# A streaming log-sum-exp: fifteen loads for seventeen, a larger first load, and late row sums on VectorE

## The chip, the core and the metric

The kernel runs on one core of a Trainium2 chip. The metric is device time in microseconds (us) of one execution: the median of the kernel before is 162.71 us over 3 runs (162.2 to 162.76).

A core has engines that run their own instruction lists side by side and meet at semaphores: TensorE (PE), VectorE (DVE), ScalarE (ACT), GpSimd (POOL) and SyncE (SP). Here SP issues every DMA, ScalarE computes exponentials and logarithms, VectorE sums, and TensorE does two tiny matmuls at the end. Sixteen DMA engines move the data between HBM and the on-chip memory SBUF; PSUM is a second, smaller on-chip memory.

## The reference

```python
def setup_inputs():
    batch, seq, dim = 32, 512, 1024
    return {"x": np.random.randn(batch, seq, dim).astype(np.float32), "axis": -1}

def reference(x, axis):
    x_max = np.max(x, axis=axis, keepdims=True)
    return (x_max.squeeze(axis) + np.log(np.sum(np.exp(x - x_max), axis=axis))).astype(np.float32)
```

There are 16,384 rows of 1024 float32 values, 67.1 MB, and one number comes out of each row.

## The kernel before

Each of the 128 partitions holds 128 consecutive rows of the input. "A row" below means one row in every partition: 128 x 1024 values, 0.52 MB. The kernel streams the 128 rows through a ring of 51 rows in SBUF (`ring`, `RING_ROWS`).

It takes a short cut: it computes log(sum(exp(x))) without subtracting the maximum, and then checks that every sum lay between `LOW` and `HIGH`. If one did not, a second pass (lines 320 to 343) does the work again with the maximum subtracted. With this input the second pass does not run; each engine only tests a verdict and branches to the end.

The list `CHUNKS` (lines 10 to 15) sets the order of the work. Each entry is one load: its rows, how many of them VectorE sums, into how many pieces ScalarE's exp of these rows is cut, and whether VectorE sums by halves. The loop of line 213 goes through the list:

- SP issues the load into the next free rows of the ring (`load`, line 135). Before it does, it waits until the engines that last used those rows are done. A load that does not fit before the end of the ring starts at row 0.
- ScalarE waits until the load has landed and computes exp in place (line 235), for all rows of a piece in one instruction.
- VectorE waits for this exp and sums: with one reduction for the piece (line 255), or, by halves, with one instruction per row that adds the second half of the row to the first and accumulates the sum (line 242, followed by a short read of the accumulator).
- Rows beyond the count for VectorE are summed by ScalarE while it computes exp, row by row (line 262), each followed by an accumulator read.

The loads are of 4, 15, 16, 16, 16, 14, 13, 9, 7, 5, 4, 3, 2, 1, 1, 1 and 1 rows. The last four are "late" rows (`LATE`): ScalarE sums all four, and the sums go to `late` in PSUM; all others go to `sums` in SBUF.

Logarithms are taken in three instructions (`take_logs`, line 157): of 81 columns ahead of the exp of the 9-row load (`LN_AT`, `LN_LAG`), of 43 columns ahead of the last exp (line 221), and of the four late columns at the very end (line 272). SP then stores the first 124 columns (line 276) and the four late ones (line 278). All loads and stores go through one DMA queue, q1. The first load is issued ahead of the barrier with which the program begins (lines 354 to 360).

The check on the sums is VectorE's: the largest and smallest of `sums` (lines 293 and 294), a compare of these with the bounds, a compare of the late columns (line 283, after the last Ln), two matmuls that count the good ones over all partitions (lines 304 and 307), and a reduction to one number (line 312), which SP, ScalarE and VectorE load to decide their branch. At the end SP waits for the stores.

Of the kernel before, what the change touches and what calls it, by code (L numbers as in the profile page):

```python
# [9 lines left out]
CHUNKS = [  # L10
    (4, 4, 1, False), (15, 15, 1, False), (16, 16, 2, False), (16, 16, 2, False),
    (16, 15, 2, False), (14, 14, 2, False), (13, 12, 2, False), (9, 8, 1, False),
    (7, 7, 1, True), (5, 4, 1, True), (4, 3, 1, True), (3, 3, 1, False), (2, 2, 1, True),
    (1, 0, 1, False), (1, 0, 1, False), (1, 0, 1, False), (1, 0, 1, False),
]

CUTS = ()
RING_ROWS = 51


UNEVEN = ()
PARTS = ((0, 128, 2), (1, 128, 4), (3, 128, 8), (7, 64, 8), (71, 128, 8))


LN_AT = 7
LN_LAG = 1


LATE = 4

# [8 lines left out]
def kernel(  # L39
# [6 lines left out]
    nc = tc.nc  # L46
    P = nc.NUM_PARTITIONS
# [4 lines left out]
    N, D = x_flat.shape  # L52
    assert N % P == 0
    NB = N // P
    assert sum(r for r, *_ in CHUNKS) == NB
    assert sum(STEPS) == NB
# [4 lines left out]
    Alu = mybir.AluOpType  # L61
# [4 lines left out]


    assert CHUNKS[-1][0] == 1
    spans = list(zip((0, *CUTS), (*CUTS, D)))
    assert 1 <= len(spans) <= 2  # L70
    n_late = LATE - 1 + len(spans)

# [11 lines left out]
    votes = nc.alloc_psum_tensor("votes", [P, 512], fp32).ap()  # L84
    late = nc.alloc_psum_tensor("late", [P, 512], fp32).ap()

    ALL_GOOD = P * K
    TOO_MANY = 2048.0
    assert TOO_MANY > ALL_GOOD

    landed = [nc.alloc_semaphore(f"landed{i}") for i in range(len(CHUNKS) + len(spans) - 1)]
    act_done = nc.alloc_semaphore("act_done")
# [26 lines left out]
    row = slot = 0  # L119
    for r, *_ in CHUNKS:  # L120
        if slot + r > RING_ROWS:
            slot = 0
        place.append((slot, row))
        slot += r
        row += r
# [8 lines left out]

    def load(i):
        (s, row), r = place[i], CHUNKS[i][0]
        act_wait = max(a for a, _ in busy[s : s + r])
        dve_wait = max(d for _, d in busy[s : s + r])
        if dve_wait:
            nc.sync.wait_ge(dve_done, dve_wait)  # L140
        if act_wait:
            nc.sync.wait_ge(act_done, act_wait)
        dst, src = ring[:, s : s + r], x_v[:, row : row + r]
        if i == len(CHUNKS) - 1:
            for k, (lo, hi) in enumerate(spans):
                nc.sync.dma_start(out=dst[:, :, lo:hi], in_=src[:, :, lo:hi]).then_inc(
                    landed[i + k], 16
                )
        elif i in UNEVEN:
            for first, last, step in PARTS:  # L150
                nc.sync.dma_start(
                    out=dst[first:last:step], in_=src[first:last:step]
                ).then_inc(landed[i], 16)
        else:
            nc.sync.dma_start(out=dst, in_=src).then_inc(landed[i], 16)

# [9 lines left out]

    late_row = place[-LATE][1]
    assert not any(n_dve for _, n_dve, _, _ in CHUNKS[-LATE:])

    def total(t):  # L170
# [3 lines left out]
    n_barrier = len(body.instructions)  # L174
    load(0)
    n_early = len(body.instructions)

# [31 lines left out]
    nc.gpsimd.memset(weights[:, 1:], -TOO_MANY).then_inc(pool_done, 1)  # L209

    logged = 0
    done_before = [(0, 0)]
    for i, (r, n_dve, parts, by_halves) in enumerate(CHUNKS):
        if i:
            load(i)
        s, row = place[i]
        if i == LN_AT:
            logged = place[i - LN_LAG][1]
            take_logs(0, logged, sums[:, :logged], *done_before[i - LN_LAG])
        if i == len(CHUNKS) - 1:  # L220
            take_logs(logged, late_row, sums[:, logged:late_row], *done_before[-LATE])
            early_logs = acts
            for k, (lo, hi) in enumerate(spans):
                nc.scalar.wait_ge(landed[i + k], 16)
                nc.scalar.activation(  # L225
                    out=ring[:, s, lo:hi],
                    in_=ring[:, s, lo:hi],
                    func=Exp,
                    accum_out=late[:, LATE - 1 + k : LATE + k],
                ).then_inc(act_done, 1)  # L230
                acts += 1
            continue
        nc.scalar.wait_ge(landed[i], 16 * (len(PARTS) if i in UNEVEN else 1))
        for lo, hi in cuts(n_dve, parts):
# [5 lines left out]
            if by_halves:  # L240
                for j in range(lo, hi):
                    nc.vector.tensor_tensor_reduce(  # L242
                        out=ring[:, s + j, : D // 2],
                        in0=ring[:, s + j, : D // 2],
                        in1=ring[:, s + j, D // 2 :],
                        scale=1.0,
                        scalar=0.0,
                        op0=Alu.add,
                        op1=Alu.add,
                        accum_out=sums[:, row + j : row + j + 1],  # L250
                    ).then_inc(dve_done, 1)
                    dves += 1
                    busy[s + j] = (0, dves)
            else:
                nc.vector.reduce_sum(  # L255
                    out=sums[:, row + lo : row + hi], in_=ring[:, s + lo : s + hi], axis=AX
                ).then_inc(dve_done, 1)
                dves += 1
                for j in range(lo, hi):
                    busy[s + j] = (0, dves)  # L260
        for j in range(n_dve, r):
# [7 lines left out]
            busy[s + j] = (acts, 0)  # L269
        done_before.append((dves, acts))  # L270

    take_logs(late_row, NB, late[:, : NB - late_row], dves, acts)


    nc.sync.wait_ge(act_done, early_logs)
    nc.sync.dma_start(out=out_v[:, :late_row], in_=res[:, :late_row]).then_inc(stored, 16)
    nc.sync.wait_ge(act_done, acts)
    nc.sync.dma_start(out=out_v[:, late_row:], in_=res[:, late_row:]).then_inc(stored, 16)


    def compare(lo, hi, values):
        nonlocal dves
        nc.vector.tensor_tensor(  # L283
            out=above[:, :, lo:hi],
            in0=values.unsqueeze(1).to_broadcast([P, 2, hi - lo]),
            in1=bounds[:, :, lo:hi],
            op=Alu.is_gt,
        ).then_inc(dve_done, 1)
        dves += 1

    nc.vector.wait_ge(act_done, done_before[-LATE][1])
    nc.vector.wait_ge(dve_done, dves)
    nc.vector.reduce_max(out=ends[:, :1], in_=sums[:, :late_row], axis=AX).then_inc(dve_done, 1)  # L293
    nc.vector.tensor_reduce(  # L294
        out=ends[:, 1:], in_=sums[:, :late_row], axis=AX, op=Alu.min
    ).then_inc(dve_done, 1)
    dves += 2
    nc.vector.wait_ge(pool_done, 1)
    nc.vector.wait_ge(dve_done, dves)
    compare(0, 2, ends)  # L300
# [95 lines left out]
```

## Time and profile before

| | |
|---|---|
| median of 3 runs | 162.71 us (162.2 to 162.76) |
| the profiled execution | 162.67 us |
| its span | 161.3 us |
| HBM read, written | 67.11 MB, 0.07 MB: 416 GB/s over the span |
| VectorE busy | 121.9 us (76%), 51 instructions |
| ScalarE busy | 115.1 us (71%), 40 instructions |
| VectorE waiting for exps | 37.2 us, four times, longest 23.3 us |
| ScalarE waiting for loads | 43.9 us, eight times, longest 14.7 us |
| SP waiting for VectorE before loads | 122.8 us, seven times, longest 52.7 us |
| issue of the first load, of the last | 0.00 us, 130.07 us |

The profile covers one execution. The span runs from the first instruction shown to the last; the time of the execution is longer by what lies outside it. Lines name an engine, the kernel's line (L235), the operation, the tile written and the tile read with the shape (partitions x elements); then busy time and the mean of one, or, in the timeline, start and duration, and in brackets the idle time before with what ended it. "SPq" is SP issuing a DMA: the issue takes a fraction of a microsecond, the transfer goes on in the DMA engines, and the time to landing is told separately. An engine's wait costs something only if it delays what ends last.

### The profile page before, as it was taken

How to read it: one execution, taken by the hardware profiler on the slowest of the kernel's cores; microseconds unless marked ns; L12 is line 12 of the kernel's file. 1: busy time of each engine (PE TensorE's matmuls, PEld its weight loads, DVE VectorE, ACT ScalarE, POOL GpSimd, SP SyncE). 2: the span in 40 equal slices, each digit the busy share in tenths (PEclk: the TensorE clock that was granted, in tenths of full speed). 3: DMA queues.
4: the chain of work that ended last, by engine and by line, in shares of the span. 5: the costliest groups of instructions: out<-in, count | busy, mean ns of one | idle time of the engine just before them, and what ended most of it. 6: DMA issues, size and time to landing. Idle time of an engine off the chain costs nothing.

```text
span 161.3 us, 149 instructions
## 1 busy us (share of the span) xinstructions
PE 0.2 (0%) x2; PEld 0.1 (0%) x2; DVE 121.9 (76%) x51; ACT 115.1 (71%) x40; POOL 0.4 (0%) x8
## 2 busy tenths in 40 slices
PE   0000000000000000000000000000000000000000
PEld 0000000000000000000000000000000000000000
DVE  0028000003999999999999699999999999999884
ACT  3170005996079960999419993999199999999996
POOL 1000000000000000000000000000000000000000
DMA  7999799979979989989979999999999999999991
GB/s 256 508 488 442 305 472 520 439 341 520 439 341 520 423 358 520 423 358 520 423 325 455 455 455 439 423 423 423 412 402 430 436 420 410 427 436 412 417 407 42
DMA packets 2737, 67.18 MB, mean 417 GB/s; under 512 B 560, under 2 KB 560, under 8 KB 1072
## 3 DMA queue, kind: packets, MB, share of 16 engines
q1 hardware_dynamic: 2736, 67.18, 97.4%
q14 instruction: 1, 0.01, 0.0%
HBM read 67.11 MB, written 0.07 MB: 416 GB/s over the span
## 4 chain that ended last, share of the span: by engine, by line
DMA 49%; DVE 30%; ACT 20%; issue 0%; PE 0%
DMA ring<-in_x_dram 49%; DVE sums L255 29%; ACT ring L235 17%; ACT ring L262 3%; ACT ring L225 1%; ACT res L162 0%; DVE above L283 0%; PE votes L304 0%; DVE verdict L312 0%; PE votes L307 0%
## 5 line engine op out<-in xcount | busy, mean ns | idle before, releaser
L255 DVE TENSOR_REDUCE sums<-ring 128x8 f32<-128x8192 f32 (+5 forms) x14 | 111.2, 7994 | 37.3 <-ACT ring L235 37.2
L235 ACT ACTIVATE ring<-ring 128x8192 f32<-128x8192 f32 (+6 forms) x18 | 104.4, 5836 | 43.9 <-DMA ring<-in_x_dram 43.9
L242 DVE CUSTOM_DVE_ANT_0 ring<-ring 128x512 f32<-128x512 f32 x16 | 9.9, 684 | 0.0
L262 ACT ACTIVATE ring<-ring 128x1024 f32<-128x1024 f32 x8 | 8.2, 1041 | 0.0
L205 ACT ACT_TABLE_LOAD x1 | 1.3, 1283 | 0.8 <-PEq L377 0.8
L262 ACT ACTIVATION_READ_ACCUMULATOR ring<-ring 128x1 f32 x8 | 1.4, 174 | 0.0
L242 DVE DVE_READ_ACCUMULATOR2_ANT sums<- 128x1 f32 x16 | 1.3, 80 | 0.0
L225 ACT ACTIVATE ring<-ring 128x1024 f32<-128x1024 f32 x1 | 1.0, 1040 | 0.0
L283 DVE TENSOR_TENSOR above<-late,bounds 128x8 bf16<-128x8 f32 x1 | 0.2, 168 | 0.7 <-ACT res L162 0.7
L162 ACT ACTIVATE res<-sums 128x81 f32<-128x81 f32 (+1 forms) x2 | 0.5, 248 | 0.0
L312 DVE TENSOR_REDUCE verdict<-votes 1x1 int32<-1x6 f32 x1 | 0.2, 152 | 0.3 <-PE votes L307 0.3
L293 DVE TENSOR_REDUCE ends<-sums 128x1 f32<-128x124 f32 x1 | 0.3, 282 | 0.1
L304 PE MATMUL votes<-above,weights 128*1 128x6 bf16 x1 | 0.2, 167 | 160.0 <-DVE above L283 160.0
L294 DVE TENSOR_REDUCE ends<-sums 128x1 f32<-128x124 f32 x1 | 0.3, 271 | 0.0
L283 DVE TENSOR_TENSOR above<-ends,bounds 128x4 bf16<-128x4 f32 x1 | 0.2, 162 | 0.1
L162 ACT ACTIVATE res<-late 128x4 f32<-128x4 f32 x1 | 0.2, 173 | 0.0
L304 PEld LDWEIGHTS votes<-above,weights 128*1 128x1 bf16 x1 | 0.1, 80 | 160.0 <-DVE above L283 160.0
L307 PE MATMUL votes<-above,weights 128*1 128x6 bf16 x1 | 0.2, 165 | 0.0
L225 ACT ACTIVATION_READ_ACCUMULATOR ring<-ring 128x1 f32 x1 | 0.2, 153 | 0.0
L206 POOL MEMSET bounds<- 128x6 f32 x1 | 0.1, 104 | 0.4 <-POOLq L377 0.4
L207 POOL MEMSET bounds<- 128x6 f32 x1 | 0.1, 104 | 0.0
L377 POOL MEMSET const-bfloat16-1.0<- 128x1 bf16 x1 | 0.1, 103 | 0.0
(6 smaller groups left out, 0.6 us busy)
## 6 DMA issues: line engine op xcount, KB each, us to landing
ring<-in_x_dram SPq DMA_DIRECT2D x1, 7680.0 KB, 25.1
ring<-in_x_dram SPq DMA_DIRECT2D x1, 7168.0 KB, 28.6
ring<-in_x_dram SPq DMA_DIRECT2D x1, 6656.0 KB, 35.7
ring<-in_x_dram SPq DMA_DIRECT2D x1, 4608.0 KB, 20.3
ring<-in_x_dram SPq DMA_DIRECT2D x2, 2048.0 KB, 16.2
ring<-in_x_dram SPq DMA_DIRECT2D x1, 3584.0 KB, 28.5
ring<-in_x_dram SPq DMA_DIRECT2D x1, 2560.0 KB, 27.5
ring<-in_x_dram SPq DMA_DIRECT2D x4, 512.0 KB, 27.2
```

The lines of the kernel that those rows point to most:

```text
L162: nc.scalar.activation(out=res[:, lo:hi], in_=src, func=Ln, bias=bias).then_inc(act_done, 1)
L205: nc.scalar.preload_act_table_set("natural_log_exp_and_others")
L225: nc.scalar.activation(out=ring[:, s, lo:hi], in_=ring[:, s, lo:hi], func=Exp, accum_out=late[:, LATE - 1 + k : LATE + k],).then_inc(act_d ...
L235: nc.scalar.activation(out=ring[:, s + lo : s + hi], in_=ring[:, s + lo : s + hi], func=Exp).then_inc(act_done, 1)
L242: nc.vector.tensor_tensor_reduce(out=ring[:, s + j, : D // 2], in0=ring[:, s + j, : D // 2], in1=ring[:, s + j, D // 2 :], scale=1.0, scal ...
L255: nc.vector.reduce_sum(out=sums[:, row + lo : row + hi], in_=ring[:, s + lo : s + hi], axis=AX).then_inc(dve_done, 1)
L262: nc.scalar.activation(out=ring[:, s + j], in_=ring[:, s + j], func=Exp, accum_out=total(row + j),).then_inc(act_done, 1)
L283: nc.vector.tensor_tensor(out=above[:, :, lo:hi], in0=values.unsqueeze(1).to_broadcast([P, 2, hi - lo]), in1=bounds[:, :, lo:hi], op=Alu.i ...
L293: nc.vector.reduce_max(out=ends[:, :1], in_=sums[:, :late_row], axis=AX).then_inc(dve_done, 1)
L294: nc.vector.tensor_reduce(out=ends[:, 1:], in_=sums[:, :late_row], axis=AX, op=Alu.min).then_inc(dve_done, 1)
L304: nc.tensor.matmul(votes[:1, :K], lhsT=weights[:, :1], rhs=above[:, 0], start=True, stop=False)
L307: nc.tensor.matmul(votes[:1, :K], lhsT=weights[:, 1:], rhs=above[:, 1], start=False, stop=True).then_inc(counted, 1)
```

## The change

- The loads are 16 rows five times, then 13, 10, 7, 5, 4, 3 and 2 (12 entries of `CHUNKS`), and the last four rows are cut into pieces of 1.75, 1.25 and 1 row (`LAST_ROWS`, `CUTS`): 15 loads. The first has 16 rows.
- VectorE sums everything from the 10-row load on by halves, the last row apart, which ScalarE sums as it computes exp. Of the first six loads ScalarE sums four rows of the fifth and one of the sixth. The 1.75-row piece gives VectorE one row and the first three quarters of the next; the 1.25-row piece gives it that row's last quarter, which starts from the sum so far and so waits for VectorE's own last result, and one more row.
- "Late" now means everything from the 5-row load on: 18 rows. Their sums are in PSUM, 17 columns in one bank and the last, ScalarE's, at the start of the next bank.
- Logs: 64 columns ahead of the exps of the 13-row load, 46 ahead of the exp of the 4-row load, 18 at the end. The first store (110 columns) is issued once the 4-row load's exp is done, after SP has issued all loads; the second stores 18.
- Largest and smallest of `sums` are taken between the sums of the 4-row and the 3-row load. The compare, the matmuls and the verdict cover 20 columns for 6.
- VectorE's code is aligned at its start to a multiple of 128 instruction slots.

```diff
 CHUNKS = [
-    (4, 4, 1, False), (15, 15, 1, False), (16, 16, 2, False), (16, 16, 2, False),
-    (16, 15, 2, False), (14, 14, 2, False), (13, 12, 2, False), (9, 8, 1, False),
-    (7, 7, 1, True), (5, 4, 1, True), (4, 3, 1, True), (3, 3, 1, False), (2, 2, 1, True),
-    (1, 0, 1, False), (1, 0, 1, False), (1, 0, 1, False), (1, 0, 1, False),
+    (16, 16, 2, False), (16, 16, 2, False), (16, 16, 2, False), (16, 16, 2, False),
+    (16, 12, 2, False), (13, 12, 2, False), (10, 10, 1, True), (7, 7, 1, True),
+    (5, 5, 1, True), (4, 4, 1, True), (3, 3, 1, True), (2, 2, 1, True),
 ]
-CUTS = ()
+LAST_ROWS = 4
+CUTS = (1792, 3072)
-LN_AT = 7
-LN_LAG = 1
-LATE = 4
+LOGS = {5: 3, 9: 7}
+LATE = 8
...
+    n_late = LAST_ROWS + sum(r for r, *_ in CHUNKS[LATE:])
+    late_row = NB - n_late
...
-    late = nc.alloc_psum_tensor("late", [P, 512], fp32).ap()
+    BANK = 512
+    banks = nc.alloc_psum_tensor("banks", [P, 2 * BANK], fp32).ap()
+    late = banks[:, BANK + 1 - n_late : BANK + 1]
...
     load(0)
+    nc.vector.addr_align(128, max_nops=0)
...
+    def halves(s, row, lo=0, hi=D):
+        nonlocal dves
+        half = (hi - lo) // 2
+        if lo:
+            nc.vector.wait_ge(dve_done, dves)
+        nc.vector.tensor_tensor_reduce(
+            out=ring[:, s, lo : lo + half],
+            in0=ring[:, s, lo : lo + half],
+            in1=ring[:, s, lo + half : hi],
+            scale=1.0,
+            scalar=total(row) if lo else 0.0,
+            op0=Alu.add,
+            op1=Alu.add,
+            accum_out=total(row),
+        ).then_inc(dve_done, 1)
+        dves += 1
...
-        if i == LN_AT:
-            logged = place[i - LN_LAG][1]
-            take_logs(0, logged, sums[:, :logged], *done_before[i - LN_LAG])
-        if i == len(CHUNKS) - 1:
-            take_logs(logged, late_row, sums[:, logged:late_row], *done_before[-LATE])
...
+        if i in LOGS:
+            upto = place[LOGS[i] + 1][1]
+            take_logs(logged, upto, sums[:, logged:upto], *done_after[LOGS[i]])
+            logged = upto
...
+        if i == LATE + 1:
+            old_dves, old_acts = done_after[LATE - 1]
+            nc.vector.wait_ge(act_done, old_acts)
+            nc.vector.wait_ge(dve_done, old_dves)
+            nc.vector.reduce_max(out=ends[:, :1], in_=sums[:, :late_row], axis=AX).then_inc(dve_done, 1)
+            nc.vector.tensor_reduce(out=ends[:, 1:], in_=sums[:, :late_row], axis=AX, op=Alu.min).then_inc(dve_done, 1)
...
+    s, row = place[-1]
+    wait_free(s, LAST_ROWS)
+    here, there = flat(ring[:, s : s + LAST_ROWS]), flat(x_v[:, row:])
+    for k, (lo, hi) in enumerate(spans):
+        nc.sync.dma_start(out=here[:, lo:hi], in_=there[:, lo:hi]).then_inc(landed[len(CHUNKS) + k], 16)
+
+    nc.sync.wait_ge(act_done, done_after[max(LOGS)][1])
     nc.sync.dma_start(out=out_v[:, :late_row], in_=res[:, :late_row]).then_inc(stored, 16)
+    for k, (lo, hi) in enumerate(spans):
+        last = k == len(spans) - 1
+        nc.scalar.wait_ge(landed[len(CHUNKS) + k], 16)
+        nc.scalar.activation(
+            out=here[:, lo:hi], in_=here[:, lo:hi], func=Exp,
+            accum_out=total(NB - 1) if last else None,
+        ).then_inc(act_done, 1)
+        acts += 1
+        if not last:
+            nc.vector.wait_ge(act_done, acts)
+            for j in range(lo // D, -(-hi // D)):
+                halves(s + j, row + j, max(lo - j * D, 0), min(hi - j * D, D))
+
+    take_logs(late_row, NB, late[:, :n_late], dves, acts)
```

## The prediction

> **What bounds the kernel now.** I read the DMA part of the page first, because a kernel that reads each input byte once and writes almost nothing is bound by its loads if the DMA engines never rest. The first line below is the mean busy share of the 16 DMA engines in 40 slices, the third the queues.
>
> ```profile
> DMA  7999799979979989989979999999999999999991
> ...
> DMA packets 2737, 67.18 MB, mean 417 GB/s; under 512 B 560, under 2 KB 560, under 8 KB 1072
> ...
> q1 hardware_dynamic: 2736, 67.18, 97.4%
> ```
>
> Only the first and last slices are low. The sevens look like gaps, but a whole packet is counted in one slice (10 to 20 us reads 0.92, 20 to 30 us 1.14); busy time by stage settles it (stretch, length, PE, PEld, DVE, ACT, POOL, PE clock, DMA share, GB/s):
>
> ```profile
> 45.20:64.60 19.40, 0.00 (x0) 0.00 (x0) 19.40 (x3) 13.96 (x3) 0.00 (x0) 1.00 1.00 432
> 130.00:147.00 17.00, 0.00 (x0) 0.00 (x0) 16.88 (x13) 16.96 (x7) 0.00 (x0) 1.00 0.98 418
> 147.00:157.00 10.00, 0.00 (x0) 0.00 (x0) 8.87 (x22) 9.81 (x8) 0.00 (x0) 1.00 1.01 417
> 157.00:158.50 1.50, 0.00 (x0) 0.00 (x0) 1.39 (x6) 1.50 (x6) 0.00 (x0) 1.00 0.32 126
> ```
>
> The DMA is full in every stage until 157.5 us. VectorE is full too in the middle, and the chain of waits says "DVE 30%", but that is SP waiting for ring rows long before the queue runs dry. So the chain is not what I price from; when loads land is. The timeline gives landings wherever ScalarE sat waiting for one:
>
> ```profile
> 45.23 13.95 ACT L235 ACTIVATE ring<-ring 128x8192 f32<-128x8192 f32 x2 [6.35 <-DMA ring<-in_x_dram]
> 64.59 13.95 ACT L235 ACTIVATE ring<-ring 128x8192 f32<-128x8192 f32 x2 [5.41 <-DMA ring<-in_x_dram]
> 83.93 13.10 ACT L235 ACTIVATE ring<-ring 128x8192 f32<-128x8192 f32 x2 [5.39 <-DMA ring<-in_x_dram]
> 100.88 12.24 ACT L235 ACTIVATE ring<-ring 128x7168 f32<-128x7168 f32 x2 [2.81 <-DMA ring<-in_x_dram]
> 116.61 10.54 ACT L235 ACTIVATE ring<-ring 128x6144 f32<-128x6144 f32 x2 [3.49 <-DMA ring<-in_x_dram]
> ...
> 158.49 1.04 ACT L225 ACTIVATE ring<-ring 128x1024 f32<-128x1024 f32 x1
> ...
> 159.62 0.17 ACT L162 ACTIVATE res<-late 128x4 f32<-128x4 f32 x1
> 159.82 0.34 SPq L278 DMA_DIRECT2D out_dram<-res  x1
> ```
>
> Sixteen rows take 19.35 us, 13 take 15.73, so a row costs 1.207 us and a load 0.04 beside its rows. The last load is issued at 130.07 and by the DMA view lands 28.3 us later, at 158.4; the three before it land at 154.6, 155.9 and 157.2. After the last landing come one exp, one Ln, one store: 2.9 us to the span's end at 161.3. The profiled execution took 162.67 us, 1.37 outside the span, and is 0.04 below the median of 162.71.
>
> Durations come from the groups by form (busy, mean ns) and from the issue view (time to landing):
>
> ```profile
> L242 DVE CUSTOM_DVE_ANT_0 ring<-ring 128x512 f32<-128x512 f32 x16 | 9.9, 684 | 0.0
> L235 ACT ACTIVATE ring<-ring 128x3072 f32<-128x3072 f32 x2 | 5.5, 2756 | 0.2 <-DMA ring<-in_x_dram 0.2
> L235 ACT ACTIVATE ring<-ring 128x2048 f32<-128x2048 f32 x1 | 1.9, 1892 | 0.0
> L262 ACT ACTIVATION_READ_ACCUMULATOR ring<-ring 128x1 f32 x8 | 1.4, 174 | 0.0
> ...
> out_dram<-res SPq DMA_DIRECT2D x1, 2.0 KB, 1.4
> ```
>
> **The change part by part.**
>
> *Two loads fewer, 17 to 15.* From 116.6 to 158.4 are 34 rows in ten loads: 41.8 - 34 x 1.207 = 0.76, or 0.08 per load. With 0.04 from the large loads and 0.06 from the four single rows (1.27 apart), two loads are worth 0.08 to 0.16 us, all on the path. I take -0.13; the last landing moves to 158.27.
>
> The Trainium skill ("DMA: Bandwidth & Descriptors", Anatomy of one DMA, for GpSimd's path) fits a transfer as about 2.0 us plus its bytes at 436 GB/s. If that fixed part were paid load after load, two fewer would bring 4 us and the time 158.7; the rows 1.27 us apart say that it is overlapped on this queue.
>
> *The first load is 16 rows, not 4.* The first exp waits until about 22 us instead of 7.5, where the trace before has both compute engines idle (14.7 us of ScalarE's wait follow the first four rows). Nothing is lost if VectorE frees rows in time. It needs 8.68 us for 8 rows, so 17.3 per 16-row load against 19.35 of transfer. Load 3 needs load 0's rows: landed 22, first exp done at 29, sums at 46.4, while loads 1 and 2 keep the queue full until 60. The later ones (load 4 at 66 against 80, 5 at 85 against 99, 6 at 105 against 115, the last three at 127 against 153) keep 10 us or more in hand. Cost 0. The start holds an unknown: the second load (15 rows) took 18.33 us where rows and load give 18.17. That 0.16, and a like 0.18 at the 7-row load, may vanish or double: -0.35 to +0.35, and I take 0, since both kernels have such a place.
>
> *Late work, moved from ScalarE to VectorE.* I count back from 158.27: the pieces of 1.25 and 1.75 rows land at 157.00 and 155.42, the loads of 2, 3, 4, 5, 7, 10 rows at 153.24, 150.76, 147.07, 142.17, 136.07, 127.55. ScalarE: an exp is 0.18 us + 0.84 ns per element (2048 and 3072 columns), the next starting 0.1 before its end. Its ends: 136.3, 142.4, 146.7 (5 rows), 150.7, 153.5, 155.3 (2 rows), 157.13, 158.29. It is free for each landing within 0.1; the accumulator reads that it sheds (0.17 each) lay beside transfers. VectorE by halves: 0.61 us per row, start to start. Its ends: 142.5, 146.8, 149.8, wait for the exp, 153.2, 153.7 after the two reductions of `sums` (0.55, moved here from 158.4), 155.6, 156.8, wait, 158.25 after the 1.75 rows, then the wait on its own last sum (0.11 from L294 to the compare), 0.21 for the quarter row (a fixed 0.08 and 128 of 512 columns), 0.61 and 0.08: 159.34. ScalarE's last exp starts at 158.30 and its Ln can follow 1.13 later as before, at 159.43. So VectorE is ready 0.1 ahead, and Ln stands at 159.43 against 159.62: 0.13 from the loads and 0.06 because ScalarE no longer has a Ln of 43 columns (158.35) in front of the last exp.
>
> *The 46-column Ln* waits for the 7-row load's sums (146.8) while the four-row load's exp is queued behind it; that load lands at 147.07, so Ln's 0.25 is nearly covered: 0 to +0.1 there, absorbed by the gaps above. *Sums in PSUM from VectorE* have no row. ScalarE's accumulator read into PSUM takes 0.15 against 0.17 to 0.19 into SBUF, so I take 0, with bounds -0.02 and +0.1 per sum; at +0.1 the gaps of 0.9 (after 149.8) and 0.33 (after 156.8) soak up most and Ln moves by about +0.4.
>
> *Wider ends.* Ln of 18 columns for 4, +0.01. Compare of 36 elements for 8: 4 to 8 cost 6 ns, so +0.04; verdict over 20 columns, +0.02. Store landing and verdict ended together before, so I charge +0.04. *The early store* goes from 158.6 to about 150.7, on the same queue behind the last loads: 0; if it came between them, 128 packets of some 27 ns (61 of them fill 51.9% of 16 engines in 0.2 us at 159.4) are 0.2 us. SP's issues otherwise keep their order. *Aligned VectorE code* and four more memset columns lie ahead of or beside the first load: 0.
>
> Sum, on the profiled execution: 162.67 - 0.13 - 0.06 + 0.04 = 162.52.
>
> **The rivals.**
>
> *VectorE ends last by a little.* It has 0.1 us of slack at the end. At half the upper PSUM price (0.05 per sum) Ln comes 0.1 later, at the full one 0.4: 162.6 to 162.9. For it: from 127 us on VectorE has only three short gaps. Against: the 684 ns row holds through every run of pairs.
>
> *VectorE falls behind (slower).* Place: the sums from the five-row load on, all into PSUM. If each costs more than 0.13 us extra, nine of them overrun the 0.9 gap by 0.3, the five after it the 0.33 gap, and the last four add 0.5: about 1 us, 163.5 and over; at 0.2 it is 2 us, 164.6. Nothing in the profile speaks for so much; no row excludes it.
>
> *A code fetch in the tail.* VectorE's list grows from 59 to 93 entries. The instruction queue shows one packet of 0.01 MB in the span, at 159.5, taking 0.61 us (19.0% of 16 engines in 0.2 us), and nobody waited for it. One that VectorE has to wait for after 150 costs 0.6 less the slack: 163.0.
>
> The Trainium skill ("Runtime: NRT & Kernel Launch", Instruction fetch mechanics) holds that crossing a block is mostly hidden but that a taken branch out of the window stalls, which would speak against jumping to an aligned address; no run here prices such a stall, and at the program's head it would lie under the first load.
>
> *Nothing is gained.* If the time beside the rows belongs to bytes and places, not to loads, and the wide end eats the 0.06: 162.7. *The slow places vanish too*: 162.1 to 162.2.
>
> **How the numbers follow.** A measurement of this kernel tells about 0.5% (0.8 us) from no change. So same is 161.9 to 163.5. Forecast, with its neighbours that are also same: 162.52 alone 0.45, VectorE by a little 0.12, fetch 0.08, nothing gained 0.10, slow places vanish 0.05; together 0.80. VectorE behind, or a wait in the tail that I have not named, 0.13. Faster by over 0.8 us, 0.07: it needs more than the -0.6 that all favourable bounds together give, so I leave it for what the view cannot show, above all the 1.37 us outside the span. The range takes the favourable bounds and the spread of the runs shown (162.2 to 162.76) below, the full PSUM price, the store and half of that spread above: 161.9 to 163.3.
>
> **What would show it.** Right: DMA full until 157.3 to 157.4, last exp within 0.05 us of its landing at about 158.3, Ln at 159.4, last store landing 1.4 us after its issue. Wrong: a gap before a late load; a VectorE pair into PSUM above 0.65 us start to start; Ln released by VectorE well after ScalarE's last read; exps waiting for the 46-column Ln; a last landing after 158.6.

## The result and the profile after

The changed kernel takes 163.12 us (median of 9 runs, 163.0 to 163.23), the kernel before 162.22 us beside it (9 runs, 162.13 to 162.87). The ratio of the runs is 1.0040, with a 95% interval of 1.0026 to 1.0054: slower by about 0.7 us. (The medians lie 0.9 apart, because the nine runs of the kernel before fall into two groups, six at 162.13 to 162.28 and three at 162.71 to 162.87.) By the ratio that is less than the 0.5% which the prediction called the bound of what can be told, but it is clear of the interval, and it has the other sign: 162.5 was forecast, a little faster than the profiled execution. The time lies within the range given (161.9 to 163.3).

The profiled execution of the changed kernel took 163.03 us, its span 161.7. The DMA part of its page:

```profile
DMA packets 2449, 67.18 MB, mean 416 GB/s; under 512 B 528, under 2 KB 528, under 8 KB 912
...
q1 hardware_dynamic: 2448, 67.18, 96.9%
q14 instruction: 1, 0.01, 0.0%
```

Two loads fewer (each 128 packets, and 16 of 4 bytes with them) moved the same bytes, and the mean rate did not rise. Busy time by stage, with the stretches and columns of the view shown before:

```profile
45.20:64.60 19.40, 0.00 (x0) 0.00 (x0) 17.33 (x3) 14.00 (x3) 0.00 (x0) 1.00 1.01 439
130.00:147.00 17.00, 0.00 (x0) 0.00 (x0) 14.48 (x36) 16.90 (x3) 0.00 (x0) 1.00 0.99 425
147.00:157.00 10.00, 0.00 (x0) 0.00 (x0) 9.38 (x30) 9.71 (x5) 0.00 (x0) 1.00 1.00 413
```

The DMA is as full as before, and VectorE has more air in the middle. So the loss must lie ahead of the steady part or behind it. The timeline shows both ends. The kernel before began with these exps, of 4 and 15 rows:

```profile
7.54 3.62 ACT L235 ACTIVATE ring<-ring 128x4096 f32<-128x4096 f32 x1 [5.47 <-DMA ring<-in_x_dram]
...
25.88 13.00 ACT L235 ACTIVATE ring<-ring 128x15360 f32<-128x15360 f32 x1 [14.72 <-DMA ring<-in_x_dram]
```

In the changed kernel the first two lines are ScalarE's exps of the first two loads, the rest is the end:

```profile
22.48 13.95 ACT L243 ACTIVATE ring<-ring 128x8192 f32<-128x8192 f32 x2 [20.27 <-DMA ring<-in_x_dram]
...
41.83 13.95 ACT L243 ACTIVATE ring<-ring 128x8192 f32<-128x8192 f32 x2 [5.40 <-DMA ring<-in_x_dram]
...
158.49 0.14 DVE L208 DVE_READ_ACCUMULATOR2_ANT banks<- 128x1 f32 x1
158.77 0.36 DVE L208 CUSTOM_DVE_ANT_0 ring<-ring,banks 128x128 f32<-128x128 f32 x1
...
159.05 0.72 DVE L208 CUSTOM_DVE_ANT_0 ring<-ring 128x512 f32<-128x512 f32 x1
159.41 0.15 ACT L298 ACTIVATION_READ_ACCUMULATOR ring<-ring 128x1 f32 x1
159.70 0.14 DVE L208 DVE_READ_ACCUMULATOR2_ANT banks<- 128x1 f32 x1
...
159.94 0.19 ACT L153 ACTIVATE res<-banks 128x18 f32<-128x18 f32 x1 [0.38 <-DVE above L223]
```

Sixteen rows land at 22.46, where a forecast from rows and loads gives 22.0 (four rows at 7.52 in the kernel before, twelve more at 1.207); the steady part then keeps the forecast pace (19.35 per 16 rows). At the end ScalarE has read its last sum at 159.56, but the Ln starts at 159.94: it waits for VectorE's last sum, read at 159.70 to 159.85. (The view names the compare of line 223 as the releaser. That compare only stands behind VectorE's last read, and the Ln's wait names that read's semaphore.) It starts 0.09 us after the end of that read, and the 46-column Ln also started 0.09 after VectorE's sum (147.01 to 147.10); after a read of ScalarE's own the last Ln of the kernel before started within 0.03 (159.59 to 159.62).

The groups by form, VectorE's late sums and the short reads of the accumulator that follow them (a sum and its read are called a pair below):

```profile
L208 DVE CUSTOM_DVE_ANT_0 ring<-ring 128x512 f32<-128x512 f32 x33 | 21.1, 701 | 3.3 <-ACT ring L243 3.1 <-ACT ring L298 0.2
L208 DVE DVE_READ_ACCUMULATOR2_ANT banks<- 128x1 f32 x18 | 2.6, 144 | 0.0
L208 DVE DVE_READ_ACCUMULATOR2_ANT sums<- 128x1 f32 x17 | 1.4, 80 | 0.0
```

A read of the accumulator into PSUM takes 144 ns, into SBUF 80. In the timeline, pairs into PSUM start 0.648 us apart and pairs into SBUF 0.613.

Two profiled executions of each kernel (the second pair is from the controls below) divide the span like this, in us:

| | before | before, again | after | after, again | forecast |
|---|---|---|---|---|---|
| last load landed | 158.42 | 158.28 | 158.42 | 158.61 | 158.27 |
| from there to the last Ln | 1.20 | 1.21 | 1.52 | 1.53 | 1.16 |
| from the last Ln to the span's end | 1.67 | 1.66 | 1.72 | 1.72 | 1.71 |
| span | 161.29 | 161.15 | 161.66 | 161.87 | 161.15 |

In the mean the landing is 0.17 later instead of 0.13 earlier, and the Ln is 0.32 later after it. Together with 0.06 for the wider end this is 0.54, most of the 0.7 of the runs.

### The profile page after: what moved, and what is told of

The parts are those of the page before. It is cut to its first block, busy times and chain, and to the rows that moved or that the text cites. A ratio compares the mean times of both kernels' runs of the same rounds, so it can differ in the third digit from the quotient of the medians.

```text
span 161.7 us, 182 instructions
## 1 busy us (share of the span) xinstructions
PE 0.2 (0%) x2; PEld 0.1 (0%) x2; DVE 118.0 (73%) x87; ACT 115.1 (71%) x36; POOL 0.4 (0%) x8
## 4 chain that ended last, share of the span: by engine, by line
DMA 61%; ACT 17%; DVE 16%; another core or an unknown queue 3%; issue 0%; PE 0%; DVEq 0%
DMA ring<-in_x_dram 61%; ACT ring L243 16%; DVE sums L253 15%; DVE ring L208 1%; ACT ring L298 1%; DVE banks L208 0%; DVE above L223 0%; ACT res L153 0%; PE votes L320 0%; DVE verdict L328 0%; PE votes L323 0%; DVEq L207 0%
## 5 line engine op out<-in xcount | busy, mean ns | idle before, releaser
L243 ACT ACTIVATE ring<-ring 128x8192 f32<-128x8192 f32 (+7 forms) x18 | 104.2, 5836 | 43.4 <-DMA ring<-in_x_dram 43.3
L253 DVE TENSOR_REDUCE sums<-ring 128x8 f32<-128x8192 f32 (+1 forms) x12 | 95.1, 7970 | 38.8 <-ACT ring L243 38.8
L208 DVE CUSTOM_DVE_ANT_0 ring<-ring 128x512 f32<-128x512 f32 (+1 forms) x34 | 21.6, 697 | 3.3 <-ACT ring L243 3.1
L260 ACT ACTIVATE ring<-ring 128x1024 f32<-128x1024 f32 x5 | 5.2, 1039 | 0.0
L298 ACT ACTIVATE ring<-ring 128x1792 f32<-128x1792 f32 (+2 forms) x3 | 3.9, 1336 | 0.1
L208 DVE DVE_READ_ACCUMULATOR2_ANT banks<- 128x1 f32 x18 | 2.6, 144 | 0.0
L153 ACT ACTIVATE res<-sums 128x64 f32<-128x64 f32 (+1 forms) x2 | 0.5, 240 | 0.2 <-DVE sums L208 0.2
L274 DVE TENSOR_REDUCE ends<-sums 128x1 f32<-128x110 f32 x1 | 0.3, 266 | 0.0
L277 DVE TENSOR_REDUCE ends<-sums 128x1 f32<-128x110 f32 x1 | 0.3, 259 | 0.0
```

The costliest lines, as they stand in the source:

```text
L153: nc.scalar.activation(out=res[:, lo:hi], in_=src, func=Ln, bias=bias).then_inc(act_done, 1)
L208: nc.vector.tensor_tensor_reduce(out=ring[:, s, lo : lo + half], in0=ring[:, s, lo : lo + half], in1=ring[:, s, lo + half : hi], scale=1.0 ...
L243: nc.scalar.activation(out=ring[:, s + lo : s + hi], in_=ring[:, s + lo : s + hi], func=Exp).then_inc(act_done, 1)
L253: nc.vector.reduce_sum(out=sums[:, row + lo : row + hi], in_=ring[:, s + lo : s + hi], axis=AX).then_inc(dve_done, 1)
L260: nc.scalar.activation(out=ring[:, s + j], in_=ring[:, s + j], func=Exp, accum_out=total(row + j),).then_inc(act_done, 1)
L277: nc.vector.tensor_reduce(out=ends[:, 1:], in_=sums[:, :late_row], axis=AX, op=Alu.min).then_inc(dve_done, 1)
```

## The experiments

The theory after the result had three parts: the start (a first load of 16 rows), the code of VectorE (its alignment moves a fetch of instructions into the loads), and the tail (VectorE's sums into PSUM and the two-step row). Each experiment was timed against the kernel before on the same chip. Ratios with intervals:

| kernel | ratio to before |
|---|---|
| changed kernel; again | 1.0040 (1.0026 to 1.0054); 1.0044 (1.0031 to 1.0057) |
| kernel before, again | 1.0011 (1.0000 to 1.0022) |
| changed, code not aligned | 1.0063 (1.0049 to 1.0077) |
| changed, first load cut into 4 and 12 rows | 1.0042 (1.0028 to 1.0055) |
| changed, late sums in SBUF | 1.0035 (1.0022 to 1.0048) |
| changed, last four rows in four loads | 1.0031 (1.0020 to 1.0041) |
| changed, all four undone | 1.0018 (1.0008 to 1.0028) |
| before, first loads of 16 and 3 rows | 1.0016 (1.0006 to 1.0025) |
| before, code aligned | 1.0018 (1.0010 to 1.0027) |
| before, first loads of 8 and 11 rows | 1.0011 (0.9997 to 1.0026) |
| before, first load of 2 rows, sixth of 16 | 1.0097 (1.0082 to 1.0113) |
| before, first load of 2 rows, VectorE's share kept | 1.0031 (1.0021 to 1.0041) |

The kernel before against itself gives 1.0011, so steps of 0.001 (0.16 us) are not told apart by the times, and a ratio of 1.0016 or 1.0018 is only partly clear of it. There the landings in the traces carry the argument; the last landing itself differs by 0.14 and 0.19 us between two profiles of one kernel.

**The controls.**

> The kernel before, unchanged, as a control beside the other kernels of this job. Its runs so far fall between 162.1 and 163.0 with a profiled one at 162.67, so the profile that the prediction used may be one of its slower executions. If it is, a second profile lands its last load up to 0.4 us earlier than 158.42 (the row places that lost 0.16 and 0.18 us are then gone); if not, it lands within 0.1 us of it, and the runs spread for a reason that lies outside the span.

> The changed kernel, unchanged, as a control beside the other kernels of this job. Expected 0.6 to 0.9 us over the kernel before; last landing at 158.4 to 158.6; the last Ln 1.50 to 1.54 us after it (1.20 in the kernel before).

The second profile of the kernel before lands its last load at 158.28, 0.14 earlier than the first, and loses its time in other places: the second load (18.14 us) and the 7-row load (8.52) are normal this time, while a 16-row load takes 19.59. So these losses change place from run to run. The 0.14 lies between the two cases of the expectation and decides neither. The changed kernel behaves as expected: 158.61, and 1.53 to the Ln.

**The first load alone, in the kernel before.**

```diff
-    (4, 4, 1, False), (15, 15, 1, False), (16, 16, 2, False), ...
+    (16, 16, 2, False), (3, 3, 1, False), (16, 16, 2, False), ...
```

> The kernel before with its first loads of 4 and 15 rows replaced by 16 and 3; nothing else differs. Theory (the size of the first load costs by itself): 19 rows land 0.3 to 0.4 us later and the time rises from 162.2 to about 162.6. Rival: the time stays at 162.2, and the start of the changed kernel has another cause.

The issue view (KB are left out for this size; the last column is us to landing):

```profile
ring<-in_x_dram SPq DMA_DIRECT2D x1, 22.6
```

Nineteen rows landed at 26.22 instead of 25.85 and 25.67 in the two profiles of the kernel before, the last load at 158.69 instead of 158.42 and 158.28, and the time rose by 0.26 us. The theory holds for the landings. The size in time is less sure: an unchanged kernel showed 0.18 us against itself, and the profiled execution (162.96) is 0.2 above the median of its runs.

What differs is the last of the 16 DMA engines. With 16 KB packets (a first load of 4 rows, five profiles) the last one begins its first packet at 1.7 to 2.1 us, with 64 KB packets (16 rows, six profiles) at 2.1 to 2.8. First packets are slow at either size: 0.6 to 1.6 us for a usual 0.61 with 16 KB, 2.4 to 3.4 for a usual 2.42 with 64 KB. Both can be put in one number: the end of an engine's first packet less the usual time of such a packet. For the last engine that is 2.2 to 2.3 us with 16 KB in all five profiles and 2.5 to 2.9 with 64 KB in all six. Why large first packets make the last engine late was not found.

**The alignment alone, in the kernel before.**

```diff
     load(0)
+    nc.vector.addr_align(128, max_nops=0)
     n_early = len(body.instructions)
```

> The kernel before with the alignment of VectorE's code and nothing else. Theory (the alignment moves an 8 KB code packet from 159.5 us, after the loads, into the first microseconds, where it takes a DMA engine 0.3 to 0.5 us from the loads): with the small first load the engine it hits becomes the last, the first load lands at 8.0 to 8.2 instead of 7.5, all later landings move with it, and the time rises by 0.3 to 0.6 us. Rival (the fetch is absorbed by engines that finish early, and the cut first load of the earlier run was late for another reason): the first load lands at 7.5 to 7.6 and the time stays.

The instruction queue of the kernel before between 159.4 and 159.6 us; then, of this kernel, the issue view of the first load and the instruction queue between 3.0 and 3.5 us:

```profile
q14 instruction: 1, 0.01, 19.0%
```

```profile
ring<-in_x_dram SPq DMA_DIRECT2D x1, 2048.0 KB, 8.1
```

```profile
q14 instruction: 1, 0.01, 4.0%
```

The one 8 KB instruction packet of the span now runs at 3.11 us, in the loads, and no longer at 159.5 after them. It takes 0.32 us, and the 16 KB load packet that starts as it ends takes 1.13 us instead of 0.61, so the engine that carries both loses over 0.8 us. (The records name no engine; the times fit end to start.) Fifteen engines are done with the first load at 6.83 to 7.39 us, one at 8.08. The first load lands at 8.08 instead of 7.52, 19 rows at 26.25, the last load at 158.63; the time rises by 0.29 us, or 0.2 against the control beside it. This was the theory, at the lower end of its range or just below. The difference shrinks from 0.56 us at the first load to 0.2 or 0.35 at the last: a load has landed when the last engine is done, so once one engine is far behind (1.2 to 1.3 us after the first in every later load), slow packets of the other 15 need no longer show. This reading was not tested by itself.

**The changed kernel without the alignment.**

```diff
     load(0)
-    nc.vector.addr_align(128, max_nops=0)
     n_early = len(body.instructions)
```

> The changed kernel without the alignment of VectorE's code; nothing else differs. In the changed kernel's trace an instruction packet of 8 KB runs on one DMA engine at 4.2 us and the load packet beside it takes 2.96 us instead of 2.42; that engine is the last of the 16 to finish the first load, 0.16 us after the next. Theory (three separate costs: a late start from the large first load, sums into PSUM, and the code fetch): the fetch leaves the start, the first load lands at 22.3 instead of 22.46, the time falls by 0.1 to 0.2 us, to about 162.95. Rival (the alignment causes the whole late start): the first load lands at 22.0 and the time falls by 0.45 us. Second rival (without it VectorE waits for code in the tail): the time rises by 0.3 us or more, with a gap in VectorE's late pairs.

It became slower, not faster: 1.0063 against 1.0040 and 1.0044. The first load landed at 22.48, so the 16-row start is late without any fetch. What the fetch at 4.2 us adds to it varies. The changed kernel's instruction queue between 4.1 and 4.6 us:

```profile
q14 instruction: 1, 0.01, 3.9%
```

In all four profiles with a 16-row load and aligned code (the two of the changed kernel and two below) it falls on an engine that began early, at 1.2 us. That engine loses 0.85 us and finishes the first load last, 0.12, 0.46, 0.12 and 0.42 us after the next; the load lands at 22.46 to 22.73.

Without the alignment the packet came at 146.43. VectorE showed no gap, but a load did: the 3-row load took 3.90 us after the 4-row load (3.69 in the changed kernel), and ScalarE waited for it:

```profile
147.24 3.60 ACT L242 ACTIVATE ring<-ring 128x4096 f32<-128x4096 f32 x1
...
151.12 2.76 ACT L242 ACTIVATE ring<-ring 128x3072 f32<-128x3072 f32 x1 [0.28 <-DMA ring<-in_x_dram]
```

The expected sign was wrong. The second rival named the sign but not the way: it is not VectorE that waits for its code, it is the load that shares a DMA engine with it (the packet behind the code took 1.12 us for 0.46). The trace shows 0.21 us of the 0.3 to 0.4 by which this kernel is slower than the changed one. It is of the fastest of the six runs, and its last load lands at 158.60, no later than in the changed kernel's second profile; where the rest goes is not shown.

**The changed kernel with a first load of 4 rows.**

```diff
-    (16, 16, 2, False), (16, 16, 2, False), (16, 16, 2, False), (16, 16, 2, False),
+    (4, 4, 1, False), (12, 12, 2, False),
+    (16, 16, 2, False), (16, 16, 2, False), (16, 16, 2, False),
...
-LOGS = {5: 3, 9: 7}
-LATE = 8
+LOGS = {6: 4, 10: 8}
+LATE = 9
```

> The changed kernel with its first load of 16 rows cut into 4 and 12 (16 loads instead of 15; the logs stay at the same rows). Theory (64 KB per partition in the first load make the DMA engines start up to 0.45 us later and slower): the first load lands at 7.5 as in the kernel before, 16 rows are in by 22.1 instead of 22.46, and the time falls by 0.3 us less 0.07 for the load, to about 162.8 to 162.9. Rival (the late start belongs to the alignment or varies from run to run): no gain, 163.1 to 163.2.

No gain: 163.15 us, 1.0042. Four rows landed at 8.15 and 16 at 22.69, later than in the changed kernel (22.46 and 22.66). With the alignment in it, the instruction packet came at 3.18, and the small first load is hit as in the aligned kernel before. Fifteen of the engines had the 16 rows in by 21.99, as the theory has it; the one behind the code came 0.7 later. So the theory's number failed because the two start costs are not a sum: each puts some engine behind, and the last engine decides.

**Late sums in SBUF.**

```diff
-    BANK = 512
-    banks = nc.alloc_psum_tensor("banks", [P, 2 * BANK], fp32).ap()
-    late = banks[:, BANK + 1 - n_late : BANK + 1]
+    late = nc.alloc_sbuf_tensor("late", [P, n_late], fp32).ap()
```

> The changed kernel with the 18 late sums in SBUF instead of PSUM. Theory (the PSUM destination makes VectorE's sums slow: reads of the accumulator of 0.144 us for 0.080, pairs 0.648 apart for 0.613): reads fall to 0.08, VectorE's last sum ends about 0.3 us earlier, the last Ln is released by ScalarE or within 0.1 us of it, and the time falls by 0.25 to 0.35 us, to about 162.8. Rival (the chain of the last two pieces is too long whatever its destination, because the quarter row waits for its own predecessor): Ln moves by 0.1 us or less.

The groups by form, and the last Ln:

```profile
L206 DVE CUSTOM_DVE_ANT_0 ring<-ring 128x512 f32<-128x512 f32 x33 | 20.6, 689 | 3.8 <-ACT ring L241 3.3 <-ACT ring L296 0.5
L206 DVE DVE_READ_ACCUMULATOR2_ANT late<- 128x1 f32 x18 | 1.5, 83 | 0.0
```

```profile
159.83 0.22 ACT L151 ACTIVATE res<-late 128x18 f32<-128x18 f32 x1
```

Reads fell to 83 ns, and the Ln followed the last landing (158.51) by 1.32 us instead of 1.52. So 0.2 us of the tail is PSUM, and VectorE still ends last, by 0.05 us. An Ln that reads SBUF took 0.22 us for 0.19, so the end gained 0.17: less than expected. By the times the gain is 0.0005 to 0.0009, not told from none.

**The last four rows in four loads.**

```diff
-CUTS = (1792, 3072)
+CUTS = (1024, 2048, 3072)
```

> The changed kernel with the last four rows in four loads of one row instead of pieces of 1.75, 1.25 and 1 row; sums stay in PSUM, no row is summed in two steps. Theory (VectorE's last two pieces and the wait between them make the Ln late): VectorE's last sum ends 0.4 us before ScalarE's last read, the Ln follows the last landing by 1.15 to 1.2 us instead of 1.52, and with one load more (0.07) the time falls by 0.25 to 0.3 us against the changed kernel. Rival (the PSUM destination alone is the cost, and VectorE is behind from the five-row load on): VectorE still ends last and the time falls by less than 0.1 us.

The end of the timeline:

```profile
158.86 1.06 ACT L298 ACTIVATE ring<-ring 128x1024 f32<-128x1024 f32 x1 [0.15 <-DMA ring<-in_x_dram]
159.36 0.14 DVE L208 DVE_READ_ACCUMULATOR2_ANT banks<- 128x1 f32 x1
...
159.83 0.15 ACT L298 ACTIVATION_READ_ACCUMULATOR ring<-ring 128x1 f32 x1
160.01 0.19 ACT L153 ACTIVATE res<-banks 128x18 f32<-128x18 f32 x1
```

VectorE now ends 0.48 us before ScalarE, and the Ln follows the landing (158.84) by 1.17 us, with the sums still in PSUM. The time is 0.0013 of 162.5, or 0.21 us, below the changed kernel timed beside it (162.81 to 163.13 against 163.03 to 163.28; the intervals of the two ratios overlap). That is a little less than expected, and the profile, of the slowest run, shows no gain in the span: its loads land late (16 rows at 22.73, the last at 158.84). The theory of the tail holds: the two-step row and PSUM together keep the Ln waiting, and taking away either the slow destination (0.20) or the order of pieces (0.36) takes back some or all of it.

**All four undone at once.** The changed kernel with the four edits above: not aligned, first loads of 4 and 12 rows, late sums in SBUF, last four rows in four loads (17 loads).

> The changed kernel with every suspected cost taken out at once: no alignment, first load of 16 rows cut into 4 and 12, late sums in SBUF, the last four rows in four loads of one row (17 loads). Theory (the start and the tail are the whole loss, and VectorE's longer list brings its code fetch into the loads): the first load lands at 7.5 to 7.6 and 16 rows at 22.2 or earlier, the last Ln follows the last landing by 1.15 to 1.2 us, a code packet runs at about 146 us and delays the loads after it by up to 0.2 us; time 0 to 0.3 us over the kernel before. Rival (something else in the change costs, such as the halves, the early store or the rows given to each engine): it stays 0.5 us or more over the kernel before.

At 1.0018 it lies 0.3 us over the kernel before, the upper end of the theory and well below the rival's 0.5. The head is cured: four rows at 7.39, 16 at 21.90, half a microsecond ahead of the changed kernel, and still 0.48 ahead when the 5-row load lands (141.86 for 142.34). The tail is cured: 1.20 us to the Ln. But the code packet came at 142.22, and the next load took 5.42 us for 4.89:

```profile
147.30 6.45 ACT L241 ACTIVATE ring<-ring 128x4096 f32<-128x4096 f32 x2 [0.39 <-DMA ring<-in_x_dram]
```

The landing of a load is recorded once for each DMA engine, and these records show it: the 16 engines finish the 5-row load within 0.62 us of one another, the 4-row load within 1.15. The load packet behind the code took 1.23 us for 0.61; its engine ends 0.5 us behind the next, and all later loads wait for it, to 158.56. So with VectorE's longer list the fetch falls among the loads in one place or another: at 4 us if the code is aligned, at 142 to 146 if not. In the kernel before it comes at 159.5, when all loads are in: it falls into the first store, which lands at 160.85 (160.39 in the aligned kernel before), and the second store lands after that in any case.

**Other sizes of the first load.** Both are the kernel before:

```diff
-    (4, 4, 1, False), (15, 15, 1, False), (16, 16, 2, False), (16, 16, 2, False),
-    (16, 15, 2, False), (14, 14, 2, False), ...
+    (2, 2, 1, False), (15, 15, 1, False), (16, 16, 2, False), (16, 16, 2, False),
+    (16, 15, 2, False), (16, 16, 2, False), ...
```

> The kernel before with a first load of 2 rows instead of 4; the two rows go to the sixth load (16 for 14). Theory (larger packets at the start make the last engine start later): 17 rows land no later than by the rows and the load alone, at about 23.4 (25.8 less two rows), and the time stays or falls by up to 0.1 us. Rival (a small first load leaves too little work before the second): 17 rows land later than 23.6 and the time rises.

```diff
-    (4, 4, 1, False), (15, 15, 1, False), ...
+    (8, 8, 1, False), (11, 11, 1, False), ...
```

> The kernel before with first loads of 8 and 11 rows for 4 and 15. Theory: the cost lies between none and that of 16 rows (0.26 us): 19 rows land at 25.9 to 26.1 and the time rises by 0.05 to 0.2 us. Rival (a step, at packets of 64 KB alone): 19 rows land at 25.7 to 25.85 as in the kernel before.

With eight rows the profiled execution (163.35, at the upper end of 162.57 to 163.7) lost 0.8 us in its second load, and the ratio's interval holds 1: by the time this is inconclusive. The start is less so. The end of the last engine's first packet less the usual time of such a packet is 2.5 us here (32 KB, usually 1.21), between the 2.2 to 2.3 of 16 KB and the 2.5 to 2.9 of 64 KB, and 1.9 in the two kernels that begin with two rows (8 KB, usually 0.31): so this start grows with the first load. What it is worth in time these three kernels do not tell.

With two rows the loads went as hoped or better, 17 rows at 22.86 and the last load at 157.96, 0.3 to 0.5 earlier than in the kernel before. Yet the time rose by 1.5 us. The end of its timeline:

```profile
159.38 0.08 DVE L242 DVE_READ_ACCUMULATOR2_ANT sums<- 128x1 f32 x1
159.55 0.24 ACT L162 ACTIVATE res<-sums 128x43 f32<-128x43 f32 x1 [1.57 <-DVE sums L242]
...
159.70 1.04 ACT L225 ACTIVATE ring<-ring 128x1024 f32<-128x1024 f32 x1
```

The two rows moved to the sixth load, where VectorE has no time to spare. It ended its sums 1.2 us later, the 43-column Ln waited for them, and the last exp stood behind that Ln for 1.7 us with its data landed. To test the head without this, the next kernel keeps VectorE's share:

```diff
-    (4, 4, 1, False), (15, 15, 1, False), (16, 16, 2, False), (16, 16, 2, False),
-    (16, 15, 2, False), (14, 14, 2, False), ...
+    (2, 2, 1, False), (16, 16, 2, False), (16, 16, 2, False), (16, 16, 2, False),
+    (16, 15, 2, False), (15, 14, 2, False), ...
```

> The kernel before with a first load of 2 rows, and the rest arranged so that VectorE has no more to do than in it: loads of 2, 16, 16, 16, 16, 15 and 13 rows for 4, 15, 16, 16, 16, 14 and 13, the added row of the sixth summed by ScalarE, everything after unchanged. Theory (the first 2-row run gained 0.3 to 0.4 us at the start and lost it because VectorE fell behind and the 43-column Ln held the last exp): 18 rows land at about 24.1, the last load at 157.9 to 158.1, the last exp starts within 0.1 us of it, and the time falls by 0.2 to 0.4 us below the kernel before. Rival (the early landing in that run had to do with the slow finish of its rows, not with the head): the last load lands at 158.3 to 158.4 and the time stays.

```profile
24.10 13.95 ACT L235 ACTIVATE ring<-ring 128x8192 f32<-128x8192 f32 x2 [17.42 <-DMA ring<-in_x_dram]
43.63 13.95 ACT L235 ACTIVATE ring<-ring 128x8192 f32<-128x8192 f32 x2 [5.58 <-DMA ring<-in_x_dram]
63.27 13.95 ACT L235 ACTIVATE ring<-ring 128x8192 f32<-128x8192 f32 x2 [5.69 <-DMA ring<-in_x_dram]
82.80 13.10 ACT L235 ACTIVATE ring<-ring 128x8192 f32<-128x8192 f32 x2 [5.58 <-DMA ring<-in_x_dram]
```

It was not faster but slower, 1.0031. Eighteen rows landed at 24.08, as the theory has it, but then 16 rows took 19.53 to 19.64 us three times instead of 19.35, and the last load landed at 158.45. The span, 161.0 to 161.4 over 12 runs, is about that of the kernel before beside it (160.7 to 161.6). The rest of the loss is outside the span: 1.69 to 1.78 us in every run, against 1.31 to 1.42 in every run of the two kernels. Neither the slow large loads nor the 0.4 us outside are explained. No kernel tried here beats the kernel before.

## Why the prediction was wrong

- **What bounds the kernel** was right: the DMA stays full in the steady part, the landings follow 1.207 us per row, and all that moved lies in the first 25 us, the last 3, and in one packet.
- **Two loads fewer** was right in its pace (112 rows and 14 loads after the first landing took 135.96 us; 112 x 1.207 and 14 x 0.065 give 136.09) and worthless in the sum.
- **What failed**: by the two pairs of profiles the span grew by 0.54 us where it was to shrink by 0.15. Of these 0.69, about 0.30 are the landing, 0.36 the way from there to the last Ln, and 0.02 the wider end.
- **The first load is 16 rows: "Cost 0"** is the step that failed first. I asked only whether the compute engines lose something while they wait, and took the start of the DMA engines as the same in both kernels. It is not: the 16-row load alone, in the kernel before, lands 19 rows 0.4 to 0.55 us later and the last load 0.3 to 0.4, at a time 0.26 higher, of which the control leaves up to 0.18 in doubt.
- **"Aligned VectorE code ... lie ahead of or beside the first load: 0"** failed in the same way. I had seen the instruction packet at 159.5 and priced it as a wait of VectorE. It costs as a packet on one of the 16 DMA engines: 0.2 to 0.3 us alone in the kernel before. In the changed kernel the late 16-row start covers part of it: its engine finishes the first load last by 0.12 to 0.46. Without the alignment the packet comes near the end and the kernel is slower still, by more than its trace explains. The rival of a code fetch in the tail did not come in the changed kernel; where the fetch did come late, a load waited for it, not VectorE.
- These two, which do not simply add, are what the runs show behind a landing of +0.17 instead of the forecast -0.13. How the 0.30 divides between them is open.
- **VectorE "0.1 ahead" at the end** was wrong in its size. The PSUM sums, taken at 0, cost 0.035 per pair and 0.064 in the last read, inside the bounds given; with them VectorE's last sum is 0.2 later. The slack itself was not there: 159.34 for VectorE against 159.43 for the Ln leaves out the 0.09 us from VectorE's read to ScalarE's Ln that the trace after shows. The wait of the quarter row on its own last sum and its short instruction took 0.43 (158.63 to 159.05) where 0.32 was worked out. Together the Ln follows the landing by 1.52 instead of 1.16: of these 0.36, 0.2 are PSUM, 0.1 the quarter row, and the rest is not accounted for. An Ln that VectorE releases well after ScalarE's last read is a sign of being wrong that the prediction named. The rival "VectorE ends last by a little" is what came, at nearly the 0.4 that it gave for its full price, though the price per sum was a third of that; it had 0.12 of the chance. That its size fits is luck, since PSUM gave only 0.2 of it.
- **VectorE falls behind (slower)** did not come: 0.035 per sum is far from the 0.13 at which it decides, and VectorE has gaps until 157.4.
- **The wider ends** (+0.04) measured 0.06. **The early store** was free: issued at 150.9, it landed at 158.61, just behind the last load (158.42). **The 46-column Ln** held the 4-row load's exp by nothing that showed (147.26 for a landing at 147.24).
- **The base**: the profiled 162.67 is 0.4 above the median of the nine runs beside the result (162.22), so a forecast of no change from it was too high by that against these runs; beside the later kernels the median of the kernel before was 162.35 to 162.69.
- **The range** held (163.12 in 161.9 to 163.3), in part by luck: its room above was given to a PSUM price three times the measured one, to a store that cost nothing and to the spread of the runs, and none of it to the start.

## What to carry to other kernels

When the DMA engines are full, a load lands with the slowest of the engines. What puts the last one further behind is paid at once; what hits one that is ahead costs only what exceeds its lead (0.12 to 0.46 of 0.85 us at the start of the changed kernel). So price the start of the first load and every packet that is not data, a code fetch above all, not only waits of the compute engines. A longer instruction list can cost time on an engine that has time to spare, because its code comes through the same DMA engines as the loads; ask when the next block is fetched and what is in flight then. And where two chains meet at the end with 0.1 us of slack, take the slack as none: the handover between the engines alone was worth 0.09 us, the unknown destination 0.2 and the wait on the engine's own result 0.1 more than its price.

## What was not expected of the hardware

- An 8 KB instruction packet takes 0.31 us among the loads, and the load packet behind it is slow by 0.5 to 0.7 us as well, whatever its size (1.12 for 0.46, 1.13 and 1.23 for 0.61, 2.96 for 2.42): its DMA engine loses 0.8 to 1.0 us. The load in flight landed 0.1 to 0.7 us after what the other 15 engines had ready.
- The accumulator read of VectorE takes 144 ns into PSUM and 80 into SBUF, while ScalarE's takes 153 into PSUM and about 186 into SBUF: the two engines prefer different memories.
- The first packet of a DMA engine took up to 1.0 us longer than a usual one, with 16 KB packets as with 64 KB, and the last of the engines was under way later the larger the first packets were: 1.9 us for 8 KB, 2.2 to 2.3 for 16, 2.5 for 32, 2.5 to 2.9 for 64.
- One arrangement of loads in the kernel before added 0.4 us outside the span in all 12 of its runs, for no reason that the profile shows.
